# A diffusion step's front: the prompt's tokens between the two latent tiles, the first norm in two halves, small loads later, first columns and W splits in a written order

## The chip, the cores and the metric

One core of a Trainium2 chip runs the whole step. The metric is the device time of one execution in microseconds (us), as a median of several runs.

## The reference

One layer (DEPTH is 1) of a hybrid diffusion backbone over 1024 latent tokens and 256 prompt tokens of width 1024, all in float32. What the change touches is the layer's beginning:

```python
def adaln(cond, w_ada, b_ada):
    m = jax.nn.silu(cond.astype(F32)) @ w_ada.astype(F32) + b_ada.astype(F32)
    return jnp.split(m[..., None, :], N_MOD, axis=-1)
...
    sh1, sc1, g1, sh2, sc2, g2 = mod
    h = rms_norm(x, norm_mix_w) * (1.0 + sc1) + sh1
...
    z = h @ w_in
    hq, hf_f, hf_b, hi, hg, aq, ak, av, gl = jnp.split(z, _split_points(), axis=-1)
    q = rms_norm(aq.reshape(b, l, N_HEADS, HEAD_DIM), q_norm_w)
    k = rms_norm(ak.reshape(b, l, N_KV, HEAD_DIM), k_norm_w)
    v = av.reshape(b, l, N_KV, HEAD_DIM)
    if latent:
        q = axial_rope(q)
        k_lat = axial_rope(k)
```

Behind it come the scan, the attention, the output projections and the MLP, which the change leaves alone. Latent and prompt tokens have their own conditioning vector (c and c_ctx) and the same weights.

## The kernel before, in words

The tokens lie in three tiles, TT: t = 0 and t = 1 are the latent ones (512 tokens, 4 blocks of 128 each), t = 2 is the prompt (256 tokens, 2 blocks). A product is made of three float32 matmuls: each operand is split into a high part (ACT) and a low part (DVE), and hi·hi, hi·lo and lo·hi are summed on PE.

The front projects the first 512 columns of w_in (half of q, all of k and v) for all tokens, while it computes the modulation on the way. Its pieces:

- `norm1_rows(t)` loads a tile's rows (tiles `xr`, on the SP queue, two halves a block), squares and sums them (on ACT with an accumulator, tile `sq`; for the second halves of tile 0 on DVE, `sqv`), adds the halves (`mm`, DVE), takes the power −0.5 (`rst`, on POOL) and scales the rows (DVE, L250, eight for a latent tile).
- `norm1_tr(t, kc)` transposes column block kc (one of KC = 8) of the scaled rows on PE into a PSUM bank `ps_t`, of which there are two (L256). `norm1_col(t, kc)` makes the column's high part `hs` on ACT (L265), the full one `xnb` on ACT (L270) or, for every third column of a latent tile, on DVE (L268), and the low part on DVE (L271). A bank is free when these have read it.
- `front_ada(j)` loads eight pieces `wa` of w_ada (256 KB each) and multiplies them with the conditioning (L530, 32 small matmuls, which the profile shows as 64 records); `ev` copies the result out of PSUM on ACT (L533). `front_late(j)` transposes it (L539) and adds the bias on DVE (L543, L544): these are scale and shift of columns 2j and 2j + 1. `front_w(kc)` loads a row block of w_in (`wst`) and splits it (ACT L277, DVE L278).
- `front_z(t, kc)` multiplies column kc of tile t: for each block hi·hi (L558) and hi·lo (L559), then for each block lo·hi (L562): 12 matmuls for a latent tile, 6 for the prompt. The sums stay in PSUM over all eight columns; then ACT evacuates them (`kve`, `qe`, L442 and L448).
- `kv_consume` and `q_consume` do for a pair of blocks the norm, the rotary part (`qb`, on POOL, and `qa`) and the splits (`vst`, `kT`, `qT`); transposes of theirs wait in a list, and `flush` issues them between PE's matmuls by a clock that the program counts itself.

The loop `for idx in range(len(steps))` goes through the 24 steps, t = 0, 1, 2 and kc = 0 to 7 in each. From the eighth step on, columns are transposed three steps ahead (AHEAD). PE executes in the order in which this code is written; the other engines' queues are ordered by a scheduler that builds them by estimated times and by priority (`high_priority` brings the columns forward). Each engine works its queue strictly in order. SP issues loads in order, too, with at most eight under way, since each waits for the one eight places before. The row pieces, `wa`, cos, sin and the cached keys share a ring of 20 buffers.

Behind the front `z_tok(AQ)` projects the other half of q, then the scan's projections and the attention follow.

Of the kernel before, what the change touches and what calls it, by code (L numbers as in the profile page):

```python
# [9 lines left out]
F32 = mybir.dt.float32  # L10
# [5 lines left out]
P = 128  # L16
# [28 lines left out]
def build(ctx, tc, I, O, C):  # L45
# [52 lines left out]
        return dp.tile(list(shape), dt, name=name)  # L98

    def dma(out, in_):  # L100
        sp.dma_start(out=f32(out), in_=f32(in_))
# [4 lines left out]
    def f32(ap):  # L106
        return ap.bitcast(F32)
# [27 lines left out]
    lbs = small((("norm_ffn_w", 8), ("final_norm_w", 8), ("hgrn_lb_logits", 16)), NFFN, g_)  # L135
    qwb = cp.tile([P, 64], F32, name="qwb")
    g_.dma_start(out=qwb, in_=I["q_norm_w"].broadcast_to([P, 64]))
    kwb = cp.tile([P, 64], F32, name="kwb")
    g_.dma_start(out=kwb, in_=I["k_norm_w"].broadcast_to([P, 64]))
    hnb = cp.tile([P, P], F32, name="hnb")  # L140
    g_.dma_start(out=hnb, in_=I["hgrn_norm_w"].broadcast_to([P, P]))
    masks = []
    for d in range(2):
        m = cp.tile([P, P], F32, name="mask%d" % d)
        g_.dma_start(out=m, in_=C["masks"][d])
        masks.append(m)

    v.tensor_scalar(qwb, qwb, 0.125, None, op0=ALU.mult)
    v.tensor_scalar(hnb, hnb, 0.5, None, op0=ALU.mult)
# [71 lines left out]
    h_first = [H(2)]  # L221
    hT = [[None] * KC for _ in range(3)]

    def norm1_rows(t):
        t0, n, cond = TT[t]
        xs = []
        ss = T(8, "ss")
        rst = T(4, "rst")
        nb = NB[t]
        for b in range(nb):  # L230
            xt = load_x(t0 // P + b)
            for i in range(2):
                acc = ss[:, 2 * b + i:2 * b + i + 1]
                if t == 0 and i == 1:

                    jk = S(name="sqv")
                    v.tensor_tensor(jk, xt[i], xt[i], op=ALU.mult)
                    v.tensor_reduce(acc, jk, axis=AX.X, op=ALU.add)
                else:
                    jk = S(name="sq")  # L240
                    s_.activation(jk, xt[i], AF.Square, accum_out=acc)
# [4 lines left out]
        v.tensor_scalar(m[:, 0:nb], m[:, 0:nb], 1.0 / D, EPS, op0=ALU.mult, op1=ALU.add)  # L246
        g_.tensor_tensor(rst[:, 0:nb], m[:, 0:nb], mexp[:, 0:nb], op=ALU.pow)
        for i in range(2):
            for b in range(nb):
                v.tensor_scalar(xs[b][i], xs[b][i], rst[:, b:b + 1], None, op0=ALU.mult)  # L250
        return xs
# [7 lines left out]
    def norm1_col(t, kc, pt):  # L259
        t0, n, cond = TT[t]  # L260
        hT[t][kc] = hi, lo = hpair(t)
        xn = xnb[:, kc % 4, :]
        sc, sh = s1[:, cond, kc:kc + 1], modc[:, cond, kc:kc + 1]
        with tc.high_priority(offset=600):
            s_.activation(hi, pt[:, 0:n], AF.Identity, scale=sc, bias=sh)  # L265

            if kc % 3 == 1 and t < 2:
                v.tensor_scalar(xn[:, 0:n], pt[:, 0:n], sc, sh, op0=ALU.mult, op1=ALU.add)  # L268
            else:
                s_.activation(xn[:, 0:n], pt[:, 0:n], AF.Identity, scale=sc, bias=sh)  # L270
# [248 lines left out]
    def front_ada(j):  # L519

        wa = [[None] * 4 for half in range(2)]
        for q in range(4):
            for half in range(2):
                x = wa[half][q] = S((P, 2, 256), name="wa")
                c0 = half * D + j * 256
                dma(x, I["w_ada"][q * 256:q * 256 + 256, c0:c0 + 256].rearrange("(k p) c -> p k c", p=P))
        pa = PS("g")
        for k in range(KC):
            for q in range(4):
                pe.matmul(pa[32 * q:32 * q + 32, 0:P], ada_l[:, k, :], wa[q // 2][k // 2][:, k % 2, (q % 2) * P:(q % 2 + 1) * P],  # L530
                          start=(k == 0), stop=(k == KC - 1))
        ev = S((P, P), name="ev", ring="F")
        s_.activation(ev, pa[:, 0:P], AF.Copy)  # L533
        return pa, ev

    def front_late(j, late):
        pa, ev = late
# [6 lines left out]
        v.scalar_tensor_tensor(s1[:, :, c], modc[:, :, 8 + 2 * j:10 + 2 * j], 1.0,  # L544
                               cols[:, NMIX + 2 * j:NMIX + 2 * j + 2].unsqueeze(1).broadcast_to([P, 2, 2]), op0=ALU.add, op1=ALU.mult)

    def front_w(kc):
        raw = S(name="wst")
        dma(raw, I["w_in"][kc * P:(kc + 1) * P, QKV:QKV + 512])
        hi, lo = w_row(kc)  # L550
        split(hi, lo, raw)

    def front_z(t, kc, banks):
        mh, ml = hT[t][kc]
        wh, wl = w_row(kc)
        for b in range(NB[t]):
            off = b * P
            pe.matmul(banks[b], mh[:, off:off + P], wh, start=(kc == 0), stop=False)  # L558
# [19 lines left out]
    rows_n = {0: norm1_rows(0)}
    lates = front_ada(0)
    front_w(0)  # L580
    front_w(1)
    pts = [norm1_tr(0, rows_n[0], kc) for kc in range(2)]
    front_late(0, lates)
    steps = [(t, kc) for t in range(3) for kc in range(KC)]
    for kc in range(2):
        norm1_col(0, kc, pts[kc])
        due(0.6)
    done, evs, w_aq = KC, [], []
    for idx in range(len(steps)):
        while idx >= KC - 1 and done <= min(idx + AHEAD, len(steps) - 1):  # L590
            t, kc = steps[done]
            norm1_col(t, kc, norm1_tr(t, rows_n[t], kc))
            due(0.6)
            done += 1
        if idx == 5:
            rows_n[1] = norm1_rows(1)
            dma(cosb, C["cos"].rearrange("(b p) d -> p b d", p=P))
            dma(sinb, C["sin"].rearrange("(b p) d -> p b d", p=P))
# [267 lines left out]
    class HUnit:  # L866
# [8 lines left out]
        def prep(self):  # L875
# [951 lines left out]
```

## Time and profile before

| | us |
|---|---|
| runs | 2057.93, 2056.11, 2056.02 |
| median | 2056.11 |
| profiled execution, its own time | 2055.24 |
| its span | 2053.1 |
| PE busy | 2012.3 |
| first projection of the front (PE, L558) begins | 24.00 |
| first matmul behind the front (PE, L325) begins | 104.35 |

A row of the timeline has start, duration, engine, line, operation, output and inputs, and in brackets how long the engine had been idle and what ended that. PE is TensorE's matmul, PEld its weight load, DVE VectorE, ACT ScalarE, POOL GpSimd, SPq the queue of SyncE, which issues loads. Durations of instructions that follow each other overlap a little, so that the cost of one is better read from start to start.

### The profile page before, as it was taken

To read this page: it belongs to the slowest core of one execution; us is meant where nothing else is said; L and a number is where in the kernel's file an instruction comes from. 1 tells how busy PE (TensorE), PEld (TensorE's weight loads), DVE (VectorE), ACT (ScalarE), POOL (GpSimd) and SP (SyncE) were. 2 spreads that over 40 slices of the span, in tenths; PEclk is the share of its full clock that TensorE was granted. 3 is DMA by queue.
4 is the path that set the end of the run, shared out by engine and by line. 5 is a ranking of instruction groups with operands and counts; after the bars stand their busy time and mean duration, and the time that the engine had idled before them with its cause. 6 is when DMAs were issued, how large, how long until landed. Compare 5 with 4: busy or idle time off the path is not lost.

```text
span 2053.1 us, 33691 instructions
## 1 busy us (share of the span) xinstructions
PE 2012.3 (98%) x12470; PEld 1736.1 (85%) x12470; DVE 1405.3 (68%) x2655; ACT 938.5 (46%) x1906; POOL 546.1 (27%) x566
## 2 busy tenths in 40 slices
PE   6899999999999999999999999999999999999998
PEld 5798889988889988888888889998888888888886
DVE  4876776777776788779254634886666666577686
ACT  4735555555555423332321335655455544333443
POOL 1473333333332265545112101222122110000130
PEclk9999999999999999999999999999999999999999
DMA  9453220322211455455544533864444489455764
GB/s 309 150 187 97 78 77 27 108 86 78 78 45 65 132 175 167 153 173 159 196 138 149 180 113 116 259 186 151 157 147 157 145 292 361 148 159 176 232 238 142
DMA packets 220052, 317.38 MB, mean 155 GB/s; under 512 B 18504, under 2 KB 139168, under 8 KB 219888
## 3 DMA queue, kind: packets, MB, share of 16 engines
q1 hardware_dynamic: 207216, 275.05, 41.7%
q0 software_dynamic: 12672, 40.18, 5.5%
q8 instruction: 98, 1.61, 0.3%
q14 instruction: 66, 0.54, 0.1%
HBM read 229.43 MB, written 85.74 MB: 154 GB/s over the span
## 4 chain that ended last, share of the span: by engine, by line
PE 62%; DVE 2%; issue 1%; ACT 0%; DMA 0%; POOL 0%; POOLq 0%; ACTq 0%; DVEq 0%
PE ps_g L308 5%; PE ps_g L309 5%; PE ps_g L310 5%; PE ps_g L1614 2%; PE ps_g L1616 2%; PE ps_g L1615 2%; PE ps_s L1460 2%; PE ps_s L1461 2%; PE ps_s L1459 2%; PE ps_s L1614 2%; PE ps_s L1615 2%; PE ps_s L1616 2%; PE ps_t L1614 2%; PE ps_t L1615 2%; PE ps_t L1616 2%; PE ps_s L308 2%
## 5 line engine op out<-in xcount | busy, mean ns | idle before, releaser
L308 PE MATMUL ps_g<-hs,wsp 128*128 128x512 f32 (+1 forms) x896 | 322.2, 360 | 1.1 <-DVE adas L186 1.0
L310 PE MATMUL ps_g<-hs,wsp 128*128 128x512 f32 (+1 forms) x896 | 309.3, 345 | 0.0
L309 PE MATMUL ps_g<-hs,wsp 128*128 128x512 f32 (+1 forms) x896 | 309.1, 345 | 0.0
L716 POOL TENSOR_SCALAR pexp<-pexp,rs 128x512 f32<-128x512 f32 (+1 forms) x104 | 171.5, 1655 | 364.8 <-ACT pTh L741 210.6
L277 ACT ACTIVATE wsp<-wraw 128x1024 fp32r<-128x1024 f32 x110 | 109.7, 997 | 276.6 <-PE ps_g L309 82.8
L278 DVE TENSOR_TENSOR wsp<-wraw,wsp 128x1024 fp32r<-128x1024 f32 x110 | 139.9, 1272 | 114.8 <-ACT wsp L277 114.4
L308 PEld LDWEIGHTS ps_g<-hs,wsp 128*128 128x128 f32 x896 | 169.6, 189 | 22.3 <-issue 4.6
L310 PEld LDWEIGHTS ps_g<-hs,wsp 128*128 128x128 f32 x896 | 169.3, 189 | 21.5
L309 PEld LDWEIGHTS ps_g<-hs,wsp 128*128 128x128 f32 x896 | 169.9, 190 | 14.8
L741 ACT ACTIVATE pTh<-ps_t 128x512 fp32r<-128x512 f32 x200 | 118.4, 603 | 124.5 <-PE ps_t L738 124.4
L277 ACT ACTIVATE ah<-ar 128x640 fp32r<-128x640 f32 (+1 forms) x112 | 80.9, 723 | 185.1 <-PE ps_g L1615 102.3
L698 DVE TENSOR_REDUCE mx<-ps_s 128x1 f32<-128x512 f32 (+1 forms) x208 | 137.1, 663 | 37.7 <-PE ps_s L697 36.9
L708 ACT ACTIVATE pexp<-ps_s,ngm 128x512 f32<-128x512 f32 (+1 forms) x208 | 137.4, 670 | 43.7 <-DVE ngm L702 42.9
L278 DVE TENSOR_TENSOR ah<-ar,ah 128x640 fp32r<-128x640 f32 (+1 forms) x112 | 93.1, 832 | 77.2 <-ACT ah L277 76.1
L742 DVE TENSOR_TENSOR pTl<-ps_t,pTh 128x512 fp32r<-128x512 f32 x200 | 135.9, 681 | 14.1 <-ACT pTh L741 13.9
L697 PE MATMUL ps_s<-Kl,Ql 128*128 128x512 f32 (+1 forms) x416 | 130.7, 411 | 0.7 <-ACT pexp L708 0.7
L738 PE MATMUL ps_t<-ident,pexp 128*128 128x128 f32 x800 | 120.8, 273 | 3.3 <-DVE pTl L742 1.8
L325 PE MATMUL ps_g<-wsp,hs 128*128 128x256 f32 x400 | 115.9, 290 | 0.0
L327 PE MATMUL ps_g<-wsp,hs 128*128 128x256 f32 x400 | 112.9, 282 | 0.0
L326 PE MATMUL ps_g<-wsp,hs 128*128 128x256 f32 x400 | 112.5, 281 | 0.0
L754 PE MATMUL ps_g<-pTl,Vl 128*128 128x256 f32 x400 | 105.9, 287 | 4.0 <-DVE pTl L742 4.0
L738 PEld LDWEIGHTS ps_t<-ident,pexp 128*128 128x128 f32 x800 | 93.6, 140 | 14.1 <-issue 4.0
(421 smaller groups left out, 5395.2 us busy)
## 6 DMA issues: line engine op xcount, KB each, us to landing
ar<-AF SPq DMA_DIRECT2D x112, 320.0 KB, 3.2
wraw<-in_w_ff SPq DMA_DIRECT2D x32, 1024.0 KB, 6.1
wr<-in_w_ff SPq DMA_DIRECT2D x128, 256.0 KB, 4.4
wraw<-in_w_in SPq DMA_DIRECT2D x18, 1024.0 KB, 5.7
wraw<-in_w_ada SPq DMA_DIRECT2D x16, 1024.0 KB, 5.6
AF<-a POOLq DMA_DIRECT2D x48, 256.0 KB, 2.7
AF<-t POOLq DMA_DIRECT2D x48, 256.0 KB, 2.4
wa<-in_w_ada SPq DMA_DIRECT2D x32, 256.0 KB, 5.8
```

The lines of the kernel that those rows point to most:

```text
L277: s_.activation(hi, raw, AF.Copy)
L278: return v.tensor_tensor(lo, raw, f32(hi), op=ALU.subtract)
L308: pe.matmul(out, hi[:, k, :], mh, start=(first and k == 0), stop=False)
L309: pe.matmul(out, hi[:, k, :], ml, start=False, stop=False)
L310: pe.matmul(out, lo[:, k, :], mh, start=False, stop=(last and k == kcs - 1))
L697: pe.matmul(pq[:, 0:n], self.qh[:, q0:q0 + P], K[self.g][var][self.kts[i]], start=(var == 0), stop=(var == 1))
L698: v.tensor_reduce(self.mx[j][:, i:i + 1], pq[:, 0:n], axis=AX.X, op=ALU.max)
L708: s_.activation(e[:, 0:n], self.ps.pop((j, i))[:, 0:n], AF.Exp, bias=self.mx[j], accum_out=self.sm[j][:, i:i + 1])
L716: NORM[(i + j) % len(NORM)].tensor_scalar(x, x, self.rs[j], None, op0=ALU.mult)
L738: pe.transpose(pt[:, a, j * P:(j + 1) * P], self.Ps[j][i][:, b * P:(b + 1) * P], ident)
L742: v.tensor_tensor(lo, pt, f32(hi), op=ALU.subtract)
L1614: pe.matmul(bank, ph, wh, start=first and i == 0, stop=False, **more)
```

## The change

- The order of the tiles is 0, 2, 1 (`ORDER`): the prompt's eight steps stand between the latent tiles. Its PSUM banks are two "g", those of tile 1 three "s" and a "g".
- `norm1_rows` works on a list of blocks and returns the scaling as a function. Tile 0 is done in two halves of two blocks, each with its own power. The prompt's second halves are squared on DVE. The prompt's rows are called at the sixth step, behind the last column of tile 0, the second latent tile's at the eighth.
- In `front_ada(0)` the first two columns' transposes stand before the last eight of its matmuls (`mid`). At the eighth step the prompt's first two columns are transposed between hi·lo and lo·hi.
- The first two W splits are written with `issue_after`: this keeps an instruction behind another one in its engine's queue. ACT has ev, W hi 0, column 0, column 1, W hi 1; DVE has the scale, W lo 0, then the columns and W lo 1.
- c and c_ctx are loaded on POOL's queue instead of SP's; the q and k norm weights after the second power of tile 0; hnb, the masks and three small vectors after the prompt's power; the two scan states after sin (behind the cached keys and values).

ACT's queue at the squares of the second latent tile. Before, with buffer numbers (`sq_582` to `sq_608` are the eight squares of tile 1, `sq_665` is the prompt's first, `hs_649` and `hs_654` are the last two columns of tile 0):

```order
L241 ACTIVATE sq_582,ss_576<-xr_578 128x512
L241 ACTIVATE sq_584,ss_576<-xr_579 128x512
L241 ACTIVATE sq_590,ss_576<-xr_586 128x512
L533 ACTIVATE ev_566<-ps_g_533 128x128
L241 ACTIVATE sq_592,ss_576<-xr_587 128x512
L241 ACTIVATE sq_598,ss_576<-xr_594 128x512
L265 ACTIVATE hs_649<-ps_t_624,modc_127,s1_130 128x512
L270 ACTIVATE xnb_150<-ps_t_624,modc_127,s1_130 128x512
L241 ACTIVATE sq_600,ss_576<-xr_595 128x512
L265 ACTIVATE hs_654<-ps_t_629,modc_127,s1_130 128x512
L241 ACTIVATE sq_606,ss_576<-xr_602 128x512
L241 ACTIVATE sq_608,ss_576<-xr_603 128x512
```

Now (the squares of tile 1 are `sq_680` to `sq_706`, the third to the eighth stand here; `hs_874` to `hs_913` are columns 4 to 7 of the prompt, 256 wide):

```order
L267 ACTIVATE hs_874<-ps_t_871,modc_116,s1_119 128x256
L272 ACTIVATE xnb_139<-ps_t_871,modc_116,s1_119 128x256
L239 ACTIVATE sq_688,ss_674<-xr_684 128x512
L267 ACTIVATE hs_887<-ps_t_884,modc_116,s1_119 128x256
L272 ACTIVATE xnb_139<-ps_t_884,modc_116,s1_119 128x256
L239 ACTIVATE sq_690,ss_674<-xr_685 128x512
L267 ACTIVATE hs_900<-ps_t_897,modc_116,s1_119 128x256
L272 ACTIVATE xnb_139<-ps_t_897,modc_116,s1_119 128x256
L239 ACTIVATE sq_696,ss_674<-xr_692 128x512
L267 ACTIVATE hs_913<-ps_t_910,modc_116,s1_119 128x256
L272 ACTIVATE xnb_139<-ps_t_910,modc_116,s1_119 128x256
L239 ACTIVATE sq_698,ss_674<-xr_693 128x512
```

The squares have moved from under the last columns of tile 0 to between the prompt's columns; two more follow this piece. The first two squares stand ahead of it, each behind two columns, with the evacuations and four `vst` of the pairs 0 and 1 and four of the cached values.

PE at the same wait. Before, the end of tile 0's seventh column, the transposes of three columns of tile 1, and the eighth column:

```order
L562 MATMUL ps_s<-wsp,hs 128x512 x3
L562 MATMUL ps_g<-wsp,hs 128x512
L256 MATMUL ps_t<-ident,xr 128x128 x12
L558 MATMUL ps_s<-wsp,hs 128x512
L559 MATMUL ps_s<-wsp,hs 128x512
```

Now, the prompt's fifth step, the first transposes of tile 1 (x4), and the prompt's sixth step:

```order
L258 MATMUL ps_t<-ident,xr 128x128 x2
L568 MATMUL ps_g<-wsp,hs 128x512
L569 MATMUL ps_g<-wsp,hs 128x512
L568 MATMUL ps_g<-wsp,hs 128x512
L569 MATMUL ps_g<-wsp,hs 128x512
L574 MATMUL ps_g<-wsp,hs 128x512 x2
L258 MATMUL ps_t<-ident,xr 128x128 x4
L568 MATMUL ps_g<-wsp,hs 128x512
```

The transposes that need the second latent tile's rows stood before the last column of tile 0 and stand now before the last three steps of the prompt. The diff at its core:

```diff
-    small((("c", 8), ("c_ctx", 8)), CC, sp)()
+    small((("c", 8), ("c_ctx", 8)), CC, g_)()
...
+    def load_qk_w():
+        g_.dma_start(out=qwb, in_=I["q_norm_w"].broadcast_to([P, 64]))
+        g_.dma_start(out=kwb, in_=I["k_norm_w"].broadcast_to([P, 64]))
+
+    def load_rest():
+        g_.dma_start(out=hnb, in_=I["hgrn_norm_w"].broadcast_to([P, P]))
+        for d in range(2):
+            g_.dma_start(out=masks[d], in_=C["masks"][d])
+        return small((("norm_ffn_w", 8), ("final_norm_w", 8), ("hgrn_lb_logits", 16)), NFFN, g_)
...
-                if t == 0 and i == 1:
+                if t != 1 and i == 1:
...
+    def front_ada(j, wa=None, mid=None):
+
+        wa = wa or ada_load(j)
         pa = PS("g")
         for k in range(KC):
+            if mid and k == 6:
+                mid()
...
     AHEAD = 3
+    ORDER = (0, 2, 1)
+    rows_n = [[], [], []]
+    norms = [norm1_rows(0, bs, rows_n[0]) for bs in ((0, 1), (2, 3))]
+    wa0 = ada_load(0)
+    for i in range(2):
+        for _, f in norms:
+            f(i)
+    raws = [w_load(0), w_load(1)]
+    with tc.issue_after(norms[1][0].ins):
+        load_qk_w()
+    v.tensor_scalar(qwb, qwb, 0.125, None, op0=ALU.mult)
+    pts = []
+    lates = front_ada(0, wa0, lambda: pts.extend(norm1_tr(0, rows_n[0], kc) for kc in range(2)))
+    with tc.issue_after(lates[2].ins):
+        s_.activation(w_row(0)[0], raws[0], AF.Copy)
+    scales = front_late(0, lates)
+    hs0 = norm1_col(0, 0, pts[0])
+    with tc.issue_after(scales.ins):
+        v.tensor_tensor(w_row(0)[1], raws[0], f32(w_row(0)[0]), op=ALU.subtract)
+    hs1 = norm1_col(0, 1, pts[1])
+    with tc.issue_after(hs1.ins):
+        s_.activation(w_row(1)[0], raws[1], AF.Copy)
...
     for idx in range(len(steps)):
-        while idx >= KC - 1 and done <= min(idx + AHEAD, len(steps) - 1):
...
+        if idx >= KC:
+            ahead(idx + AHEAD)
...
-            banks = [PS(x) for x in ("sssp", "ggss", "sp")[t]]
+            banks = [PS(x) for x in ("sssp", "sssg", "gg")[t]]
...
+        front_z(t, kc, banks, (lambda: ahead(idx + 2)) if idx == KC - 1 else None)
...
+            if kc == KC - 3:
+                with tc.issue_after(made.ins), tc.issue_after(scales.ins):
+                    powed, f = norm1_rows(2, (0, 1), rows_n[2])
+                f(0)
+                f(1)
...
+        if idx == KC - 1:
+            with tc.issue_after(made.ins):
+                _, f = norm1_rows(1, (0, 1, 2, 3), rows_n[1])
+            f(0)
+            f(1)
+            dma(cosb, C["cos"].rearrange("(b p) d -> p b d", p=P))
+            loaded = dma(sinb, C["sin"].rearrange("(b p) d -> p b d", p=P))
+            with tc.issue_after(powed.ins):
+                lbs = load_rest()
...
-                dma(self.st, I["state_hgrn"][d, h])
+                with tc.issue_after(loaded.ins):
+                    dma(self.st, I["state_hgrn"][d, h])
```

More of the change, by code (lines that the diff above doesn't have):

```diff
@@ L100, in dma @@
     def dma(out, in_):
-        sp.dma_start(out=f32(out), in_=f32(in_))
+        return sp.dma_start(out=f32(out), in_=f32(in_))
     def store(out, in_):
@@ L131, in small @@
         return late
-    small((("c", 8), ("c_ctx", 8)), CC, sp)()
+    small((("c", 8), ("c_ctx", 8)), CC, g_)()
     small((("b_ada", 48), ("norm_mix_w", 8)), B_ADA, g_)()
-    lbs = small((("norm_ffn_w", 8), ("final_norm_w", 8), ("hgrn_lb_logits", 16)), NFFN, g_)
     qwb = cp.tile([P, 64], F32, name="qwb")
-    g_.dma_start(out=qwb, in_=I["q_norm_w"].broadcast_to([P, 64]))
     kwb = cp.tile([P, 64], F32, name="kwb")
-    g_.dma_start(out=kwb, in_=I["k_norm_w"].broadcast_to([P, 64]))
     hnb = cp.tile([P, P], F32, name="hnb")
[L141 to L149, printed above, removed]
+    masks = [cp.tile([P, P], F32, name="mask%d" % d) for d in range(2)]
+    def load_qk_w():
[6 more added lines that the diff above has]
+        return small((("norm_ffn_w", 8), ("final_norm_w", 8), ("hgrn_lb_logits", 16)), NFFN, g_)
     ada_l = cp.tile([P, KC, 32], F32, name="ada_l")
@@ L222, in build, with norm1_rows @@
     hT = [[None] * KC for _ in range(3)]
-    def norm1_rows(t):
+    def norm1_rows(t, blocks, xs):
         t0, n, cond = TT[t]
-        xs = []
+        b0, nb = blocks[0], len(blocks)
         ss = T(8, "ss")
         rst = T(4, "rst")
-        nb = NB[t]
-        for b in range(nb):
+        for b in blocks:
             xt = load_x(t0 // P + b)
             for i in range(2):
-                acc = ss[:, 2 * b + i:2 * b + i + 1]
-                if t == 0 and i == 1:
+                acc = ss[:, 2 * (b - b0) + i:2 * (b - b0) + i + 1]
+                if t != 1 and i == 1:
                     jk = S(name="sqv")
@@ L246, in norm1_rows, with scale @@
         v.tensor_scalar(m[:, 0:nb], m[:, 0:nb], 1.0 / D, EPS, op0=ALU.mult, op1=ALU.add)
[L247 to L251, printed above, removed]
+        powed = g_.tensor_tensor(rst[:, 0:nb], m[:, 0:nb], mexp[:, 0:nb], op=ALU.pow)
+        def scale(i):
+            for b in blocks:
+                x = xs[b][i]
+                scaled[0] = v.tensor_scalar(x, x, rst[:, b - b0:b - b0 + 1], None, op0=ALU.mult)
+        return powed, scale
+    scaled = [None]
     def norm1_tr(t, xs, kc):
@@ L264, in norm1_col @@
         with tc.high_priority(offset=600):
-            s_.activation(hi, pt[:, 0:n], AF.Identity, scale=sc, bias=sh)
+            made = s_.activation(hi, pt[:, 0:n], AF.Identity, scale=sc, bias=sh)
             if kc % 3 == 1 and t < 2:
@@ L271, in norm1_col @@
             v.tensor_tensor(lo, xn[:, 0:n], f32(hi), op=ALU.subtract)
+        return made
     ring = {"e": 0}
@@ L517, in w_row, with ada_load @@
         return wsps[kc // 2][:, kc % 2, :], wsps[kc // 2 + 2][:, kc % 2, :]
-    def front_ada(j):
+    def ada_load(j):
         wa = [[None] * 4 for half in range(2)]
@@ L532, in front_ada @@
         ev = S((P, P), name="ev", ring="F")
-        s_.activation(ev, pa[:, 0:P], AF.Copy)
-        return pa, ev
+        return pa, ev, s_.activation(ev, pa[:, 0:P], AF.Copy)
     def front_late(j, late):
-        pa, ev = late
+        pa, ev, _ = late
         pt = pa[:, P:2 * P]
@@ L559, in front_z @@
             pe.matmul(banks[b], mh[:, off:off + P], wl, start=False, stop=False)
+        if mid:
+            mid()
         for b in range(NB[t]):
@@ L577, in build, with ahead @@
     AHEAD = 3
[L578 to L587, printed above, removed]
+    ORDER = (0, 2, 1)
[20 more added lines that the diff above has]
+        s_.activation(w_row(1)[0], raws[1], AF.Copy)
+    with tc.issue_after(scales.ins):
+        v.tensor_tensor(w_row(1)[1], raws[1], f32(w_row(1)[0]), op=ALU.subtract)
+    due(1.2)
+    steps = [(t, kc) for t in ORDER for kc in range(KC)]
     done, evs, w_aq = KC, [], []
-    for idx in range(len(steps)):
-        while idx >= KC - 1 and done <= min(idx + AHEAD, len(steps) - 1):
+    made = None
+    def ahead(until):
+        nonlocal done, made
+        while done <= min(until, len(steps) - 1):
             t, kc = steps[done]
-            norm1_col(t, kc, norm1_tr(t, rows_n[t], kc))
+            made = norm1_col(t, kc, norm1_tr(t, rows_n[t], kc))
             due(0.6)
             done += 1
[L595 to L598, printed above, removed]
+    for idx in range(len(steps)):
+        if idx >= KC:
+            ahead(idx + AHEAD)
         t, kc = steps[idx]
@@ L604, in build @@
                 dma(raw_aq[j], I["w_in"][j * 256:j * 256 + 256, AQ:AQ + 256].rearrange("(k p) c -> p k c", p=P))
-        if t == 2 and kc in (4, 6):
+        if idx >= 2 * KC and kc in (4, 6):
             w_aq.append((wsp((P, 4, 256)), wsp((P, 4, 256))))
@@ L613, in build @@
         if kc == 0:
-            if t > 0:
+            if idx > 0:
                 front_prep(evs)
-            banks = [PS(x) for x in ("sssp", "ggss", "sp")[t]]
-        cols_next = t == 0 and kc % 2 == 1 and kc < KC - 1
+            banks = [PS(x) for x in ("sssp", "sssg", "gg")[t]]
+        cols_next = idx < KC - 1 and kc % 2 == 1
         if cols_next:
             pts = [norm1_tr(0, rows_n[0], kc + i) for i in (1, 2)]
-            front_late((kc + 1) // 2, lates)
-        front_z(t, kc, banks)
+            scales = front_late((kc + 1) // 2, lates)
+        front_z(t, kc, banks, (lambda: ahead(idx + 2)) if idx == KC - 1 else None)
         if cols_next:
             for i in (1, 2):
-                norm1_col(0, kc + i, pts[i - 1])
+                made = norm1_col(0, kc + i, pts[i - 1])
                 due(0.6)
-        elif t == 0 and kc < KC - 2:
+            if kc == KC - 3:
[3 more added lines that the diff above has]
+                f(1)
+        elif idx < KC - 2:
             lates = front_ada(kc // 2 + 1)
@@ L635, in build @@
     front_prep(evs)
+    v.tensor_scalar(hnb, hnb, 0.5, None, op0=ALU.mult)
     lbs()
```

14 lines of the change are left out of this document (7 added, 7 removed).

## The prediction

> **What bounds the kernel now.** I read the page first. TensorE (PE) is busy for nearly the whole span, so a change can only win PE's idle time, or lose by adding some.
>
> ```profile
> PE 2012.3 (98%) x12470; PEld 1736.1 (85%) x12470; DVE 1405.3 (68%) x2655; ACT 938.5 (46%) x1906; POOL 546.1 (27%) x566
> ```
>
> That leaves 2053.1 − 2012.3 = 40.8 us idle. Next I read the waits of PE for the first 110 us, the front.
>
> ```profile
> PE ps_g L530 <- DVE qwb L148: 8.9, 1, 8.9
> PE ps_t L129 <- ACT ident L113: 5.5, 1, 5.5
> PE ps_s L558 <- ACT hs L265: 2.1, 1, 2.1
> PE ps_t L256 <- ACT xnb L270: 2.0, 2, 1.2
> PE ps_t L256 <- DVE xr L250: 1.4, 1, 1.4
> PE ps_t L256 <- DVE kT L278: 1.2, 2, 0.8
> PE ps_t L256 <- DVE xnb L268: 0.5, 1, 0.5
> ```
>
> The columns are total, times, longest. The first three lie before the first projection. The last four lie between the first latent tile's last column and the end of the front: 2.0 + 1.4 + 1.2 + 0.5 = 5.1 us. The first name misleads: qwb is a tiny instruction, and what really comes last is shown by the timeline.
>
> ```profile
> 0.74 0.41 SPq L124 DMA_DIRECT2D rows<-in_c  x1
> ...
> 1.55 3.67 SPq L101 DMA_DIRECT2D xr<-in_x_sample  x8
> ...
> 20.10 0.63 PE L530 MATMUL ps_g<-wa,ada_l 128*32 128x128 f32 x12 [0.33 <-DMA wa<-in_w_ada]
> ...
> 24.00 0.50 PE L558 MATMUL ps_s<-wraw,hs 128*128 128x512 f32 x1 [2.08 <-ACT hs L265]
> ...
> 28.10 1.30 ACT L277 ACTIVATE wraw<-wst 128x512 fp32r<-128x512 f32 x2 [2.81 <-DMA wst<-in_w_in]
> ...
> 28.32 2.14 PE L530 MATMUL ps_g<-wa,ada_l 128*32 128x128 f32 x64
> ...
> 30.56 0.28 ACT L533 ACTIVATE ev<-ps_g 128x128 f32<-128x128 f32 x1 [1.15 <-PE ps_g L530]
> ...
> 31.34 0.48 PE L558 MATMUL ps_s<-wraw,hs 128*128 128x512 f32 x1
> ```
>
> PE and ACT wait for loads (wa at 20.10, wst at 28.10). The stretches tell why.
>
> ```profile
> 9.00:13.00 4.00, 0.00 (x0) 0.00 (x0) 1.66 (x5) 1.44 (x4) 0.00 (x0) 1.00 1.01 249
> 13.00:24.00 11.00, 6.30 (x73) 3.60 (x73) 6.66 (x18) 2.15 (x5) 1.14 (x2) 1.00 1.08 352
> 24.00:28.40 4.40, 4.40 (x16) 3.05 (x20) 2.17 (x3) 1.59 (x3) 0.00 (x0) 0.65 1.09 364
> 31.30:54.00 22.70, 22.70 (x221) 18.55 (x219) 9.53 (x20) 15.62 (x33) 0.29 (x1) 1.00 1.01 319
> ```
>
> After length come PE, PEld, DVE, ACT, POOL busy, the granted clock, the DMA share and GB/s. Up to 28 us the DMA engines are full; from 31.3 to 54 PE is. ACT has 22.7 − 15.6 = 7.1 us to spare in that last stretch, and the latent tile's squares lie there. That will matter.
>
> **Part by part.** *Loads and first columns.* c and c_ctx leave the SP queue, so the first row load can go where c went, 0.81 us before 1.55. These leave the opening stretch:
>
> ```profile
> mask<-const_masks POOLq DMA_DIRECT2D x2, 64.0 KB, 7.9
> ...
> hnb<-in_hgrn_norm_w POOLq DMA_DIRECT2D x1, 64.0 KB, 8.1
> qwb<-in_q_norm_w POOLq DMA_DIRECT2D x1, 32.0 KB, 6.0
> kwb<-in_k_norm_w POOLq DMA_DIRECT2D x1, 32.0 KB, 6.6
> ```
>
> That is 256 KB, 0.26 MB, at 352 GB/s 0.75 us; and the stretch in which they land ran at 249: 4 us × (352 − 249) is another 0.41 MB or 1.2 us. Together 2.7 us; the two 32 KB loads come back within the next loads and cost some 0.4 of it. From the last load of wa to the first projection it takes 24.00 − 20.10 = 3.9 us now; the eight transposes in it (1.09 in the row of 38.86 below) now run while those loads still come. So the projection starts 2.3 + 1.1 = 3.4 us earlier, at 20.6; 4.4 us of it at the clock of that stretch and the 2.14 of row 28.32 end at 27.1. ACT allows no more: the two splits of wst (28.10, 1.30 long) stand ahead of the next ev, and 2.3 us earlier they end at 27.1, so ev comes at 27.2 instead of 30.56. The projection of 31.34 comes 3.4 us earlier, and from there to 54 PE is full, so the 3.4 stays. Ends: −2.3 (the loads alone) and −4.3 (0.9 more, if the clock does not fall there and the splits' loads come sooner). **−3.4.** The state loads, moved behind cv on the SP queue, and hnb, masks and the lb rows, moved on the POOL queue to the prompt's power, are read after the front: nothing, tens of us of cover; POOL has no other work between. Were the cover gone, it would be a 4 to 8 us landing.
>
> *The latent hole closes.* The first latent tile's seventh column ends, then PE waits for the second tile's rows. The four lines above, 5.1 us; and inside the first eight transposes more is lost:
>
> ```profile
> 38.86 1.09 PE L256 MATMUL ps_t<-ident,xr 128*128 128x128 f32 x8
> ...
> 55.40 1.86 PE L256 MATMUL ps_t<-ident,xr 128*128 128x128 f32 x8 [1.38 <-DVE xr L250]
> ```
>
> 1.86 − 1.09 = 0.8. **−5.9**, ends −4 (if the late kT waits stay) and −6.
>
> *What is late next: the latent rows, in the middle of the prompt.* In the new order PE takes the first latent column's transposes after five of the prompt's eight steps, and they need all eight squares of the second latent tile. All eight are on ACT, and its queue now has them among the prompt's columns. Prices:
>
> ```profile
> 45.97 0.63 ACT L241 ACTIVATE sq<-xr 128x512 f32<-128x512 f32 x1
> ...
> 46.73 0.63 ACT L241 ACTIVATE sq<-xr 128x512 f32<-128x512 f32 x1
> ...
> 53.71 1.02 POOL L247 TENSOR_TENSOR rst<-mm,mexp 128x4 f32<-128x4 f32 x1 [37.78 <-DVE mm L246]
> ...
> 54.77 3.26 DVE L250 TENSOR_SCALAR xr<-xr,rst 128x512 f32<-128x512 f32 x8 [1.14 <-POOL rst L247]
> ...
> 58.26 0.90 ACT L435 ACTIVATE vst<-cv 128x128 fp32r<-128x128 f32 x4
> ...
> 61.46 0.38 ACT L448 ACTIVATE qe<-ps_s 128x256 f32<-128x256 f32 x1
> 61.72 0.39 ACT L442 ACTIVATE kve<-ps_s 128x256 f32<-128x256 f32 x1
> ...
> 91.78 0.44 PE L256 MATMUL ps_t<-ident,xr 128*128 128x128 f32 x2 [0.82 <-DVE kT L278]
> ...
> 93.40 0.65 ACT L265 ACTIVATE hs<-ps_t,modc,s 128x256 fp32r<-128x256 f32 x1
> ...
> 93.43 0.38 PE L256 MATMUL ps_t<-ident,xr 128*128 128x128 f32 x2
> ...
> 93.85 0.65 ACT L270 ACTIVATE xnb<-ps_t,modc,s 128x256 f32<-128x256 f32 x1
> ```
>
> From start to start: a square 0.76, an hs or xnb 0.45, an evacuation 0.26, a vst 0.2. From the prompt's first hs to the last square ACT has 16 hs and xnb (7.2), 8 squares (6.1), 8 evacuations (2.1) and 8 vst (1.6): 17.0 us in one queue. Behind it come the two small DVE instructions (0.4), POOL's power to the first scale (54.77 − 53.71 = 1.06), four scales (4 × 3.26/8 = 1.6) and the transpose with its handover (0.6): 20.7 us. PE meanwhile has the small part of the last column (4 matmuls of 0.23, 0.9), the transposes of two columns (0.5) and five steps of 93.43 − 91.78 = 1.65 (8.3; six matmuls and a column's two transposes each, so 0.23 a matmul), with 0.5 until ACT frees the first bank 10.2 us. It then stands in order, with the last three prompt steps behind the wait, though these are ready. **+10.5**; ends +6.5 (if hs and xnb cost the 0.26 of an evacuation of the same width, and a square its bare 0.63: 4 us less) and +12 (1.5 more on DVE, where other work stands between).
>
> *After the hole.* The transpose bank of latent column 1 is released by DVE, which has the eight scales, then some 4 us of pairs 0 and 1 first: **+1.0**, ends 0 and 2. The trace has no such queue; the nearest row is the kT wait of 0.82 above. The hole has about 6 us without a matmul. After the thin stretch 13 to 24 the clock in the rows was 0.65 for 4.4 us, which cost 4.4 × 0.35 = 1.5 us; so here 0 to 1.5, I take **+1.0**, nearer to the only row. [...]
>
> *The stretch behind the front.* Both pairs of the second latent tile, with rotary on POOL, now fall behind the front; before, the first was half done there.
>
> ```profile
> 104.00:147.00 43.00, 42.84 (x320) 40.52 (x319) 35.66 (x65) 15.75 (x36) 34.30 (x39) 1.00 0.56 172
> ...
> 144.63 1.30 POOL L415 TENSOR_TENSOR qa<-qa,qb 128x512 f32<-128x512 f32 x1
> ...
> 146.26 0.60 PE L473 MATMUL ps_t<-ident,qa 128*128 128x128 f32 x4
> ```
>
> POOL has 43 − 34.3 = 8.7 us to spare there and a pair costs it about 8, but the last transposes come 0.3 us after their qa. I take **+0.8**, ends 0 and +4.
>
> **The sum** against the profiled execution (2055.24 us, 2.1 around its span): −3.4 − 5.9 + 10.5 + 1.0 + 1.0 + 0.8 = +4.0, 2059.2. The median of the runs is 0.9 above that execution, so 2060.1. A measurement of this kernel can tell about 0.2%, 4.1 us.
>
> **Rivals.** *ACT keeps up* (faster): the hole in the prompt closes to 5 us or less, for which ACT's 17.0 must shrink below 11.8, or the front must give its 4.3 too. Then −4.3 − 5.9 + 5 = −5.2, 2050.9. For it speaks that my pitches are from crowded stretches, where an instruction may wait unseen; against it that ACT runs without a gap there. It decides at a hole of 5 us. 0.15. *The gains and the hole cancel*: hole 7, nothing after it: −3.4 − 5.9 + 7 = −2.3, up to +1: 2053.8 to 2057.1. 0.10. *POOL becomes the bound* (much slower): its spare 8.7 us is made of short waits for DVE, so a pair more doesn't fit; the q transposes come 4 us late, the clock falls too, the hole is 12: −3.4 − 5.9 + 12 + 2 + 1.5 + 4 = +10.2, 2066.3. 0.15. That the moves aren't made can't be: the queues' orders show them.
>
> **How the numbers follow.** The forecast has 0.60, with its own range 2057 to 2063.5; it lies on the bound, so its chance is halved: 0.30 within 0.2%, 0.30 slower. With the rivals: faster 0.15, within 0.10 + 0.30 = 0.40, slower 0.30 + 0.15 = 0.45. The range 2053 to 2066 leaves out the first rival and the top of the third, some 0.2.
>
> **What would show it.** Right: the first projection near 20.5 us, the last column of the first latent tile some 3.4 earlier than 54; PE waiting 8 us or more at a transpose of xr for DVE's scale near 67 to 73 us, with the last square just before; the front's end later than 104 although it started earlier. Wrong: no wait above 3 us there; or squares on ACT that end before PE has done five prompt steps; or the front unmoved, which would leave the hole alone, +7.

## The result and the profile after

The changed kernel takes 2061.57 us (2060.67 to 2063.85, 12 runs), the kernel before on the same chip 2055.88 (12 runs): a ratio of 1.0030, 95% interval 1.0022 to 1.0037, so 5.7 us slower. The profiled execution of the changed kernel took 2063.49 us with a span of 2061.7, which is 1.9 above its median; that of before was 0.6 below its own. Two profiles therefore differ by 8.3 where the medians differ by 5.7: terms are read from profiles, worth from ratios.

The page's totals of the changed kernel:

```profile
PE 2015.8 (98%) x12470; PEld 1739.5 (84%) x12470; DVE 1405.6 (68%) x2661; ACT 937.3 (45%) x1902; POOL 549.6 (27%) x569
```

PE idles 2061.7 − 2015.8 = 45.9 us instead of 40.8, and is 3.5 us longer busy with the same 12470 instructions: part of the loss is a slower clock (granted on the mean 0.995 instead of 0.998 of full speed). PE's waits up to the end of the front:

```profile
PE ps_t L129 <- ACT ident L113: 7.8, 1, 7.8
PE ps_t L258 <- DVE xr L250: 5.4, 1, 5.4
PE ps_t L258 <- ACT xnb L272: 2.9, 3, 2.3
...
PE ps_s L568 <- ACT hs L267: 1.3, 1, 1.3
PE ps_t L258 <- DVE kT L281: 1.1, 1, 1.1
PE ps_t L427 <- DVE kT L281: 0.9, 1, 0.9
...
PE ps_t L258 <- DVE xnb L270: 0.6, 1, 0.6
```

The wait of 8.9 at the first modulation is gone. Before, four small waits (5.1) lay between the first latent tile's last column and the end of the front; now 5.4 + 2.9 stand in the prompt, and 1.1 + 0.9 + 0.6 in the second latent tile behind it. Where they lie is shown by rows of the timeline (first projection, the loads of tile 1's rows, the prompt's first high part, a wait at the prompt's columns, the last square, the scales, the transposes):

```profile
19.64 0.73 PE L568 MATMUL ps_s<-wraw,hs 128*128 128x512 f32 x1 [1.27 <-ACT hs L267]
...
38.40 5.37 SPq L101 DMA_DIRECT2D xr<-in_x_sample  x8
...
51.77 0.56 ACT L267 ACTIVATE hs<-ps_t,modc,s 128x256 fp32r<-128x256 f32 x1 [3.56 <-PE ps_t L258]
...
57.85 0.44 PE L258 MATMUL ps_t<-ident,xr 128*128 128x128 f32 x2 [2.28 <-ACT xnb L272]
...
67.38 0.63 ACT L239 ACTIVATE sq<-xr 128x512 f32<-128x512 f32 x1
...
69.65 3.26 DVE L250 TENSOR_SCALAR xr<-xr,rst 128x512 f32<-128x512 f32 x8 [0.45 <-POOL rst L245]
...
70.29 1.57 PE L258 MATMUL ps_t<-ident,xr 128*128 128x128 f32 x4 [5.38 <-DVE xr L250]
```

The first projection came 4.4 us earlier than the 24.00 of before. ACT worked from 51.77 to 68.0 without a wait, on the prompt's columns, tile 0's evacuations, some `vst` and the squares of tile 1. The rows of tile 1 had been issued from 38.40 to 43.77 and landed 4.7 to 5.4 us after their issue, so it is their place in ACT's list and not their load that makes the squares late. Then came mean, power and the first scale, and PE went on at 70.29 after 5.38 us without work. Two places show the clock (length, PE, PEld, DVE, ACT, POOL busy, granted clock, DMA share, GB/s):

```profile
70.00:74.00 4.00, 3.71 (x10) 2.69 (x11) 4.00 (x11) 1.86 (x3) 0.61 (x1) 0.50 0.00 0
...
130.00:135.00 5.00, 2.18 (x18) 1.98 (x18) 4.41 (x7) 0.00 (x0) 5.00 (x6) 1.00 0.25 82
135.00:140.00 5.00, 5.00 (x31) 5.00 (x31) 3.73 (x8) 1.78 (x4) 5.00 (x7) 0.66 0.55 180
```

The second place is the one that the forecast had priced low. In 130 to 135 POOL is busy all the time and PE 2.18 of 5 us. The rows of the rotary sum on POOL and of the transposes that need it:

```profile
133.36 1.44 POOL L418 TENSOR_TENSOR qa<-qa,qb 128x512 f32<-128x512 f32 x1
...
134.85 0.33 PE L476 MATMUL ps_t<-ident,qa 128*128 128x128 f32 x1 [2.82 <-POOL qa L418]
```

How far this pushes the work behind it is seen from the starts of two groups of matmuls: L328, the first behind the front, and L311, the first of the next weights (this group's line in the kernel before is quoted second).

```profile
L328 PE MATMUL ps_g<-wsp,hs x19: 281/283/387, 107.8 to 114.8; 128*128 128x256 f32 x19
...
L311 PE MATMUL ps_g<-hs,wsp x33: 279/389/476, 143.4 to 164.6; 128*128 128x512 f32 x25, 128*128 128x256 f32 x8
```

```profile
L308 PE MATMUL ps_g<-hs,wsp x39: 280/389/481, 135.7 to 163.9; 128*128 128x512 f32 x31, 128*128 128x256 f32 x8
```

The front ends 107.8 − 104.35 = 3.5 us later, the stretch behind it 143.4 − 135.7 = 7.7 later: 4.2 us more were lost there.

### The profile page after: what moved, and what is told of

The parts are those of the page before. It is cut to its first block, busy times and chain, and to the rows that moved or that the text cites. A ratio compares the mean times of both kernels' runs of the same rounds, so it can differ in the third digit from the quotient of the medians.

```text
span 2061.7 us, 33700 instructions
## 1 busy us (share of the span) xinstructions
PE 2015.8 (98%) x12470; PEld 1739.5 (84%) x12470; DVE 1405.6 (68%) x2661; ACT 937.3 (45%) x1902; POOL 549.6 (27%) x569
## 4 chain that ended last, share of the span: by engine, by line
PE 88%; DVE 5%; DMA 2%; ACT 2%; issue 1%; POOL 1%; SPq 0%; POOLq 0%; DVEq 0%; ACTq 0%
PE ps_g L311 8%; PE ps_g L313 8%; PE ps_g L312 8%; PE ps_s L741 4%; PE ps_t L782 4%; PE ps_g L1660 2%; PE ps_g L1661 2%; PE ps_g L1659 2%; PE ps_g L798 2%; PE ps_s L1506 2%; PE ps_s L1504 2%; PE ps_s L1505 2%; PE ps_g L797 2%; PE ps_s L312 2%; PE ps_s L311 2%; PE ps_s L313 2%
## 5 line engine op out<-in xcount | busy, mean ns | idle before, releaser
L311 PE MATMUL ps_g<-hs,wsp 128*128 128x512 f32 (+1 forms) x896 | 322.3, 360 | 1.0 <-DVE adas L184 1.0
L311 PEld LDWEIGHTS ps_g<-hs,wsp 128*128 128x128 f32 x896 | 169.7, 189 | 21.6 <-issue 4.6
L328 PE MATMUL ps_g<-wsp,hs 128*128 128x256 f32 x400 | 116.9, 292 | 0.0
```

The source lines that it names most:

```text
L311: pe.matmul(out, hi[:, k, :], mh, start=(first and k == 0), stop=False)
```

## Experiments

Eight kernels in two sets, five rounds each, with the kernel before among the runs of each set. Ratios are to the kernel before, 0.1% is 2.06 us; against it the changed kernel stands at 1.0030. The theory: the changed opening gains, and two separate queues lose more than that, ACT's (squares among the prompt's columns) and POOL's (two pairs behind the front).

**Squares on DVE**

```diff
-                if t != 1 and i == 1:
+                if i == 1:
```

> The changed kernel, with the second halves of tile 1's rows squared on DVE instead of ACT (four squares of eight). Theory, ACT's list sets the hole in the prompt: four squares at 0.76 leave it, 3.0 us; PE's wait for the scaled rows of tile 1 falls from 5.4 to about 2.4 us, the clock falls less, the front's end comes from 107.8 to about 104.5, the time is 3 to 4.5 us below the changed kernel's. Rival, DVE takes the place of ACT: four products and four sums (some 5 us) stand on DVE ahead of the prompt's scaling and of the prompt's low parts; the wait moves to an earlier place and the time is the changed kernel's or up to 3 us above it.

Measured: 2061.27 us, ratio 1.0024 (1.0015 to 1.0033). The rival came about: the front ends at 106.1 instead of the 104.5 of the theory, and the interval of the time includes the changed kernel's 1.0030. The wait of 5.4 is gone from its place, and another one stands 15 us earlier, at the prompt's first columns; a row of PE, one of DVE ahead of it, and two stretches:

```profile
55.79 1.21 PE L258 MATMUL ps_t<-ident,xr 128*128 128x128 f32 x4 [3.70 <-DVE xr L250]
```

```profile
52.51 1.26 DVE L236 TENSOR_REDUCE ss<-sqv 128x1 f32<-128x512 f32 x2
...
53.70 0.15 DVE L244 TENSOR_SCALAR mm<-mm 128x2 f32<-128x2 f32 x1
```

```profile
54.00:58.00 4.00, 2.21 (x7) 1.87 (x8) 2.87 (x10) 1.58 (x5) 4.00 (x7) 0.62 0.44 122
58.00:62.00 4.00, 4.00 (x12) 2.73 (x10) 0.94 (x3) 4.00 (x15) 0.14 (x1) 0.53 0.51 147
```

DVE's products and sums for tile 1 stand between the halves of the prompt's own mean (its second instruction only at 53.70), so the prompt's rows are scaled late, PE waits 3.70 us there, and the clock is 0.62 and 0.53 for the next 8 us. To move work off the queue that is late isn't enough; it must not stand ahead of something nearer.

**Squares two steps earlier**

```diff
                 f(0)
                 f(1)
+                _, f = norm1_rows(1, (0, 1, 2, 3), rows_n[1])
+                f(0)
+                f(1)
...
         if idx == KC - 1:
-            with tc.issue_after(made.ins):
-                _, f = norm1_rows(1, (0, 1, 2, 3), rows_n[1])
-            f(0)
-            f(1)
```

> The changed kernel with the rows of tile 1 loaded and squared right behind the prompt's, two steps earlier, so that seven of their eight squares stand on ACT ahead of the prompt's first column instead of among its columns. Theory: ACT's list from the prompt's first hs shrinks by 7 x 0.76 = 5.3 us, PE's wait for the scaled rows of tile 1 is below 1 us, the front ends near 100 to 101, the time is 2053 to 2056, about 6 to 8 us below the changed kernel's. Rival, the stretch behind the front decides: the front ends as early, but POOL and DVE have the same list for two pairs behind it, PE's transposes wait there longer by what was won, and the time stays above 2058.

Measured: 2052.84 us, ratio 0.9985 (0.9976 to 0.9993), 0.45% or 9.2 us below the changed kernel's. Waits of PE behind 54 us up to the front's end, the first matmul behind it, and the wait in the stretch behind:

```profile
PE ps_t L258 <- ACT xnb L272: 2.7, 2, 1.7
...
PE ps_t L258 <- DVE xnb L270: 1.2, 1, 1.2
```

```profile
L328 PE MATMUL ps_g<-wsp,hs x44: 280/283/387, 98.3 to 115.0; 128*128 128x256 f32 x44
```

```profile
125.36 1.12 PE L476 MATMUL ps_t<-ident,qa 128*128 128x128 f32 x4 [2.83 <-POOL qa L418]
```

The wait for the scaled rows is gone and the front ends 9.5 us earlier than in the changed kernel. So the place of the squares was its hole. The wait for POOL stays as it was, 27.1 us behind the front's end in both (125.36 − 98.3, 134.85 − 107.8): it belongs to the list behind the front and to nothing in it.

**Rotary sums on DVE**

```diff
-        (g_ if nh == 4 else v).tensor_tensor(qa, qa, qb, op=ALU.add)
+        (qadd[0] if nh == 4 else v).tensor_tensor(qa, qa, qb, op=ALU.add)
...
+    qadd[0] = v
     front_prep(evs)
+    qadd[0] = g_
```

> The changed kernel with the sums of the rotary part (qa + qb) of the q pairs that are worked behind the front on DVE instead of POOL, two of 1.3 us. Theory, POOL is the bound behind the front: the one wait of 2.8 us at the q transposes goes, and with it the clock of 0.66 that follows for 5 us (1.7 us); front unchanged at 107.8, time 2 to 4.5 us below the changed kernel's. Rival, DVE is as full there (4.4 to 5 of each 5 us): the wait stays above 1.5 us and is put down to DVE, time within 1 us of the changed kernel's.

Measured: 2058.45 us, ratio 1.0014 (1.0005 to 1.0023), 3.3 us below the changed kernel's. The wait and the two stretches:

```profile
PE ps_t L476 <- POOL qa L418: 0.7, 1, 0.7
```

```profile
130.00:135.00 5.00, 5.00 (x45) 5.00 (x44) 4.37 (x7) 1.78 (x4) 4.92 (x5) 1.00 0.41 127
135.00:140.00 5.00, 5.00 (x38) 4.71 (x37) 4.28 (x7) 2.84 (x5) 4.92 (x8) 1.00 0.59 191
```

PE is full in both, at full clock. The front ends at 107.2 here, and the second group of weights begins 31.1 us behind it; in the kernel before these were 135.7 − 104.35 = 31.4 us, in the changed kernel 143.4 − 107.8 = 35.6.

```profile
L311 PE MATMUL ps_g<-hs,wsp x37: 277/389/476, 138.3 to 164.5; 128*128 128x512 f32 x29, 128*128 128x256 f32 x8
```

So POOL's list accounts for the whole loss behind the front: 4.5 us between the two profiles, 3.3 in time.

**The old order with the changed opening, and its lookahead**

```diff
-    ORDER = (0, 2, 1)
+    ORDER = (0, 1, 2)
...
-            banks = [PS(x) for x in ("sssp", "sssg", "gg")[t]]
+            banks = [PS(x) for x in ("sssp", "ggss", "sp")[t]]
...
             if kc == KC - 3:
-                with tc.issue_after(made.ins), tc.issue_after(scales.ins):
-                    powed, f = norm1_rows(2, (0, 1), rows_n[2])
+                powed, f = norm1_rows(1, (0, 1, 2, 3), rows_n[1])
```

> The changed kernel with the tiles in the old order 0, 1, 2, the old banks and the old places of the row loads; loads, first columns and W splits stay as changed. Theory, the order of the tiles alone costs and the front's opening alone gains: first projection near 19.6, the last column of tile 0 some 4.3 us earlier than before, the old hole of about 5 us back, the first matmul behind the front near 100.2, time 3 to 4.5 us below the kernel before (about 2052). Rival, what the opening gains is lost again in the hole, because the rows of tile 1 are bound by loads or ACT and not by PE: the hole grows from 5.1 to about 9 us, the front ends near 104, and the time is that of the kernel before.

Measured: 2057.52 us, ratio 1.0007 (0.9999 to 1.0016). My theory fell: the first projection was early (19.71), but the front ended at 105.2, since the gain was lost at the border. There ACT had the evacuations ahead of the second latent column, and PE waited:

```profile
58.85 0.43 ACT L445 ACTIVATE kve<-ps_g 128x256 f32<-128x256 f32 x1
59.11 0.44 ACT L451 ACTIVATE qe<-ps_g 128x256 f32<-128x256 f32 x1
59.37 0.85 ACT L267 ACTIVATE hs<-ps_t,modc,s 128x512 fp32r<-128x512 f32 x1
```

```profile
61.12 1.11 PE L258 MATMUL ps_t<-ident,xr 128*128 128x128 f32 x4 [3.84 <-DVE xnb L270]
```

But this kernel had kept a part of the change: the next tile's first transposes stand in the middle of the eighth step, two columns of them, instead of three ahead of it. A second kernel put that back:

```diff
-        if idx >= KC:
+        if idx >= KC - 1:
             ahead(idx + AHEAD)
...
-        front_z(t, kc, banks, (lambda: ahead(idx + 2)) if idx == KC - 1 else None)
+        front_z(t, kc, banks, None)
```

> The run with the old order, and also the old place of the next tile's first transposes (three columns ahead from the eighth step on, before its matmuls, instead of two columns in its middle). So it is the kernel before with the changed opening, loads, splits and prompt's squares. Theory, the wait of 3.8 us at the border in that run came from the later transposes: it falls to about 2, the front ends near 101 to 102, time 2052 to 2053. Rival, the border is bound by the rows of tile 1 and by ACT, whatever the transposes' place: waits there sum to 7 us or more, the front ends at 104 to 105, time 2055 to 2058.

Measured: 2051.86 us, ratio 0.9979 (0.9970 to 0.9987). The theory held: there is no wait of 3.8, PE's waits there are 1.1 and less, and the front ends at 101.3. In this profile the clock stays at 1.00 through the whole front, while in that of the run before it falls at 46.89 and at 60.54 (0.61 in 46 to 50 us, 0.82 in 58 to 62); so a part of the difference between these two runs can be the clock's.

```profile
54.58 0.66 PE L258 MATMUL ps_t<-ident,xr 128*128 128x128 f32 x4 [1.10 <-ACT xnb L272]
58.95 0.65 PE L258 MATMUL ps_t<-ident,xr 128*128 128x128 f32 x4 [0.97 <-DVE xnb L270]
```

So the changed opening is worth 4.3 us (2.7 to 6.2) in the old order, and the new order with what it brings costs 1.0030 − 0.9979, some 10.5 us.

**The loads alone, in the kernel before**

```diff
-    small((("c", 8), ("c_ctx", 8)), CC, sp)()
+    small((("c", 8), ("c_ctx", 8)), CC, g_)()
...
+    with tc.issue_after(powed[0].ins):
+        load_qk_w()
...
+            with tc.issue_after(powed[2].ins):
+                lbs = load_rest()
```

> The kernel before with only the loads moved: c and c_ctx on POOL's queue, the q and k norm weights behind the first power, hnb, the masks and the lb rows behind the prompt's power, the scan states behind sin. Order, first columns and W splits stay as before. Theory of the prediction: the loads alone are worth 2.3 us at the first projection (21.7 instead of 24.0) and PE is full from there to the first latent tile's last columns, so the time is 2053 to 2054. Rival, what the run with the old order suggests: an opening that is earlier only lengthens the wait at the border between the tiles, which is set by ACT's evacuations and DVE; first projection 2 us earlier, wait at the border 2 us longer, first matmul behind the front at 104, time that of the kernel before within 1 us.

Measured: 2053.36 us, ratio 0.9984 (0.9975 to 0.9993), a gain of 3.3 us (1.4 to 5.1). The first projection, and the stretch that the small loads had shared (249 GB/s before):

```profile
19.99 0.50 PE L558 MATMUL ps_s<-wraw,hs 128*128 128x512 f32 x1 [2.07 <-ACT hs L265]
...
47.48 0.33 PE L539 MATMUL ps_g<-ident,ev 128*128 128x128 f32 x1 [3.02 <-ACT ev L533]
```

```profile
9.00:13.00 4.00, 2.36 (x21) 1.15 (x21) 2.88 (x9) 0.72 (x2) 0.96 (x1) 1.00 1.09 365
```

In this profile the first projection is 4.0 us earlier, not 2.3. That the written order of first columns and splits adds 0.35 to it (19.64) is not shown: in the eight profiles of kernels with the changed opening the first projection begins between 18.70 and 20.22. Part of the gain is lost later in this kernel, at 47.48, where ev stands on ACT behind the squares of tile 1.

**PE kept at work in the hole**

```diff
         pt = PS("t")
+        if t == 1 and kc == 0:
+            for i in range(22):
+                pe.matmul(pt, hT[2][0][0][:, 0:P], w_row(0)[0], start=True, stop=True)
```

> The changed kernel with 22 more matmuls (128x512, 0.23 us each, 5.1 us) written into the free transpose bank just ahead of the first transposes of tile 1, whose result the transposes overwrite: PE works through the hole instead of standing. Theory, the idle PE is what makes the clock fall (0.5 from 68 to 74 us): the clock stays at 1.00 from 66 to 76, the transposes still start near 70.3, the front ends some 2 us earlier (near 105.8), the time is about 2 us below the changed kernel's. Rival, the fall has another cause (or the price of the hole is the wait alone): the clock in 70 to 76 stays below 0.8, the front ends at 107.8 or later, the time is that of the changed kernel.

Measured: 2063.09 us, ratio 1.0036 (1.0024 to 1.0049); in time no gain. The clock did what the theory says:

```profile
70.00:74.00 4.00, 3.94 (x22) 3.11 (x22) 3.77 (x9) 1.69 (x3) 1.18 (x2) 1.00 0.02 4
```

The clock is 1.00 instead of 0.50, and in 68 to 70 us PE was busy for 2.00 of 2.00 us, where the changed kernel has 0.00: at this place it was PE's idle time that lowered the clock. But the front ended only 0.6 us earlier (107.2). In this execution the first projection was 0.5 later (20.15), and the clock was at 0.50 from 58.30 to 61.71, behind the wait at the prompt's first columns, where the changed kernel's had stayed at 1.00. The scaled rows came 0.6 later (70.23), and the extra matmuls, begun at 66.42, ended some 0.5 after the first of them was ready: the transposes began at 71.41, 1.1 later than in the changed kernel. And behind the front PE waited longer than before:

```profile
PE ps_t L479 <- POOL qa L421: 4.5, 2, 3.2
```

The next late queue took back what was left: the second group of weights begins at 143.3, where it was 143.4.

**Both mends**: squares two steps earlier and sums on DVE.

> Both mends together: the changed kernel with tile 1's rows loaded and squared two steps earlier, and with the rotary sums of the q pairs behind the front on DVE. Theory, two separate holes: what the two won alone (8.7 us and 3.1 us against the changed kernel) adds up, the wait of 2.8 us at the q transposes falls below 1 us, the first matmul behind the front is at 98.3, that of the second weight group near 129.5, time about 2049.5, below the kernel before by 5 to 6 us. Rival, with the front's end 9 us earlier DVE and POOL meet other work there: the wait stays above 2 us, time 2052 to 2053.

Measured: 2050.10 us, ratio 0.9972 (0.9962 to 0.9982). The two gains add up to within their intervals: by the ratios 9.2 + 3.3 = 12.5 us for each alone, 11.9 for both. The wait at the q transposes is 1.7 us, neither below 1 nor above 2. It stands at 142.43, in the second group of weights; up to that group's start the stretch behind the front takes 128.7 − 97.7 = 31.0 us.

```profile
PE ps_t L476 <- POOL qa L418: 1.7, 1, 1.7
```

This is 5.8 us (3.7 to 7.8) faster than the kernel before. From the old order with the changed opening (0.9979) it can't be told apart: the intervals overlap.

## Why the prediction was right in direction, and where it was off

Its sign, its place and its mechanism held: an earlier opening, a hole in the prompt set by ACT's list, and more lost than won. Four sizes were off, and partly cancelled; that the sum came so near is therefore in part luck. The first rival would have had the change faster at a hole of 5 us or less. The wait at the transposes came near that, 5.4, and the change was slower all the same, by the 2.9 ahead of it, the clock's estimated 2.0, and the 2.6 and 4.2 behind it.

*Loads and first columns, −3.4.* Measured −4.4 at the first projection. In its own run the change of the loads gave 4.0, not 2.3: the 8 loads of wa and the rows run at 365 GB/s from 9 to 13 us, above the 352 that I took, and PE takes the first part of the modulation there. For the transposes moved ahead I took 1.1; the 0.4 that is left for them is less than the spread of the eight profiles (18.70 to 20.22), so their worth is not shown. The clock cancels here: it was at 0.50 for 3.41 us in both, from 25.33 before and from 19.74 now. In time the opening is worth 4.3 in the old order (2.7 to 6.2), the upper end of my bound.

*The latent hole closes, −5.9.* It closed, but the border between tiles has a price of its own, which the prompt then pays: 0.47 + 2.28 + 0.18 behind ACT's evacuations and squares (the row of 57.85). With both mends PE's waits in the prompt and behind it still sum to 2.7 + 1.2 = 3.9. I had counted only 0.5 of it, within the next term.

*The new hole, +10.5.* The waits are 5.4 + 2.9 = 8.3. ACT's list was 68.0 − 51.77 = 16.2 instead of 17.0. PE's work was right: from 51.77 to 70.29 are 18.5 us, and 18.5 − 8.3 = 10.2. The rest of the error is the handover: PE starts on the first scaled row and takes the others as they come (x4 in 1.57), so four scales needn't be waited for. What I called one wait of 8 us or more is 5.4 at its place and 2.9 at the prompt's first columns. That the hole is due to the squares is shown by the run with earlier squares. The prediction's own figures for the hole didn't fit each other: 10.5 us in the sum, 8 or more as its sign, about 6 without a matmul behind which the clock would fall. And ACT's list would have to shrink below 11.5, not 11.8, for a hole of 5 (10.2 + 5 − 3.7).

*Behind the hole, +1.0 and +1.0 for the clock.* The waits for kT and xnb are 1.1 + 0.9 + 0.6 = 2.6, over my upper end of 2. The clock was at 0.50 from 67.53 to 74.35, and PE had work in 4.1 us of that, which cost an estimated 4.1 × 0.5 = 2.0, above my end of 1.5.

These first terms sum to +3.2 in the prediction. By the trace: −4.4 − 5.9 + 8.3 + 2.6 + 2.0 = +2.6, and the front's end moved by +3.5; 0.9 is in none of these terms.

*The stretch behind the front, +0.8: the step that failed in size.* The profile lost 4.2 there: 2.8 waiting and 5 × 0.34 = 1.7 at the clock that followed. The run with the sums on DVE puts it at 3.3 in time. I had reasoned from a mean: POOL had 8.7 us to spare in 43, and a pair costs about 8, so it fits. But spare time counts only up to the moment at which the result is wanted. PE's program puts the q transposes some 24 us behind the front's end, and POOL's list for two pairs needs 27.1 up to that qa. The end of the bound, +4, lies between the two. The rival that made POOL the bound named the mechanism, but with a longer hole as well. Against the sum of +4.0 the medians moved by +5.7; this term, 3.4 too small, is larger than the difference of 1.7, and the hole, 2.2 too large, hid a part of it.

## What to carry to other kernels

Before work is put between two stages, count for each in-order queue what then stands ahead of the first thing that PE will want, and by which moment; a mean of spare time over a stretch says nothing on that. A gain at the start is only kept if the next queue on the way isn't late: here the opening had won 4.3 us, ACT's list took 9.2 and POOL's another 3.3. Work has to go to a place where its engine has time before the next wanted result. The squares, given to ACT's free time ahead of the prompt, brought ACT's part back, and half of them given to DVE ahead of a nearer result didn't; the two sums given to DVE, which had time for them there, brought POOL's part back.

## What the runs showed of the hardware

In the profiles of the kernel before and of the changed one the granted clock has two values, 1.00 and 0.50. Up to 1900 us it falls in the changed kernel at 19.74, 67.53, 135.80 and 384.97, each time for 3.41 us or, at 67.53, for twice that; and these four moments lie 14, 20 and 73 times 3.41 us apart. At 0.50 the matmuls of 128x512 start every 0.43 us there (from 20.18 on), at 1.00 every 0.23 (from 27.33 on). What stands beside a fall in these profiles is a low busy time of PE in the 3.41 us before it. That stretch in the kernel before, ahead of the fall at 25.33:

```profile
21.92:25.33 3.41, 1.33 (x7) 1.11 (x7) 1.80 (x6) 2.27 (x4) 0.00 (x0) 1.00 1.09 352
```

Such stretches in the changed kernel, the first followed by 1.00 and the second by the third:

```profile
53.87:57.28 3.41, 1.71 (x8) 1.10 (x8) 1.05 (x4) 3.41 (x14) 0.00 (x0) 1.00 0.53 158
...
132.38:135.79 3.41, 0.94 (x8) 0.94 (x9) 2.67 (x3) 0.24 (x1) 3.41 (x5) 1.00 0.29 90
135.79:139.20 3.41, 3.41 (x18) 3.41 (x17) 2.85 (x5) 1.54 (x4) 3.41 (x5) 0.50 0.60 200
```

Such stretches in the run with the extra matmuls, the first followed by 0.50 and the second by the third:

```profile
54.89:58.30 3.41, 1.25 (x6) 0.68 (x4) 1.06 (x4) 3.41 (x13) 0.00 (x0) 1.00 0.58 178
...
129.98:133.39 3.41, 1.56 (x14) 1.35 (x12) 2.81 (x6) 0.00 (x0) 3.41 (x5) 1.00 0.22 77
133.39:136.80 3.41, 2.05 (x18) 2.05 (x19) 2.28 (x3) 1.32 (x4) 3.41 (x3) 1.00 0.43 120
```

Counted in steps of 3.41 us from those moments, and up to 1900 us, the two profiles of before and now have five stretches at full clock that are followed by 0.50: PE is busy for 0.39 of the one before, for 0.50, 0.23, 0.28 and 0.30 of those now. One more with 0.50 (53.87) is followed by 1.00, and so are all with 0.59 or more. In these runs the length of a wait alone doesn't tell whether a fall follows. The wait of 2.8 us in the changed kernel left PE busy for 0.28 of a stretch, and the clock fell. The wait of 3.2 us in the run with the extra matmuls lay across 133.39, left 0.46 and 0.60, and the clock stayed. The wait of 2.3 us at the prompt's first columns left 0.50 in the changed kernel and 0.37 in that run, and only there the clock fell. Nor was PE idle for all of a stretch ahead of the fall at 25.33: its longest idle time there was 2.08 us. One stretch at 0.50 costs an estimated 3.41 × 0.5 = 1.7 us where PE has work, and the wait of 2.3 us was followed by it in one execution and not in the other; a difference of that size between two single profiles needn't be one of the kernels.

Moving 256 KB of small loads in rows of 256 and 512 bytes out of the opening (two of 32 KB only some us later), with c and c_ctx off the SP queue, moved the first projection by 4.0 us in one profile, where their bytes at 352 GB/s (13 to 24 us in the kernel before) and the 0.81 of the queue make an estimated 1.6. Which of these moves gave the rest isn't shown, since one run has them all.
